# Output projection by seven products of half-size blocks in place of eight

## The chip, the cores and the metric

The kernel runs on one core of a Trainium2 chip. The metric is the device time of one execution in microseconds. The engines of the core are called here as in the profile: PE (TensorE, with PEld for its weight loads), DVE (VectorE), ACT (ScalarE), POOL (GpSimd) and SP (SyncE, which issues all DMAs of this kernel).

## The reference, cut to what matters

The kernel computes one decoder layer on a sequence of 4096 rows of 1024 float32 values. Two branches, a sliding-window attention and a gated linear attention (GLA), each give 512 columns; their concatenation goes through one output projection with a 1024x1024 matrix and a residual with layer norm.

```python
mix = jnp.einsum('bse,ed->bsd', jnp.concatenate([out_a, out_b], axis=-1), w_out[layer])
x = layer_norm(ALPHA * x + mix, ln_g[layer], ln_b[layer])
```

## The kernel before

The 4096 rows are 32 tiles of 128 (`NB` is 32). Three stages run one after the other, each a loop over the tiles: attention, GLA, output. Every float32 operand of a projection is split into two parts in the format fp32r, a rounded high part (a cast, mostly on ACT) and the rest (a subtraction, mostly on DVE), and `project` makes three matmuls for each of its eight slices of 128 input columns: high by high, high by low and low by high.

The attention stage stores its transposed result per tile in DRAM as `mixd[n][0]` (L432), the GLA stage as `mixd[n][1]` (`b_store`, L714). The weights of a stage are loaded near the end of the stage before by `load_group`, split, and kept in places of SBUF by slot and slice: slot 0 holds the attention's `wq`, then the GLA's `v`; slot 1 `wkv`, then the GLA's `q`; slot 2 the two gates in turn; slot 3 the GLA's `k`, loaded at tile 2 of the attention stage. The two column halves of the output matrix are loaded in the last GLA tile into slots 0 and 2 (L751, L765).

In the output stage a tile is loaded from `mixd` with its residual rows `xr` and split (`mh` on ACT, `ml` on DVE). For each column half PE makes 24 matmuls of 128x512 into one PSUM bank `py`, DVE adds the residual and takes the statistics. Then DVE and ACT make the factor of the norm, ACT normalises, POOL multiplies by `lg`, DVE adds `lb`, and SP stores:

```python
act.activation(y, y, AF.Identity, bias=nb_, scale=rs)
pool.tensor_tensor(y, y, lg, ALU.mult)
dve.tensor_tensor(y, y, lb, ALU.add)
sp.dma_start(out[rows, :], y)
```

PE's order of matmuls within a GLA tile is written out by hand: the steps of other tiles (`b_attn`, `b_state`, `b_update`, `b_out`, `b_store`) stand between pieces of `project`. The order in each engine's queue is fixed when the kernel is built, by a planner that takes from the instructions that are ready by its own estimate the one with the highest priority, in general the one written first. Each queue is then worked off in that order, SP's as well. Tiles of a pool share its buffers, and a pool that is opened later may use the memory of one that was closed; an instruction that writes into such a place waits until the last use of what was there.

## Time and profile before

| | us |
|---|---|
| runs, median of 3 | 1720.0 (1718.03 to 1721.3) |
| the profiled execution | 1719.78 |
| its span, first to last instruction | 1718.1 |
| mean granted clock of PE | 0.997 |

The profile shows one execution. Times in its rows are counted from the start of the span. A group of instructions has its count, its busy time and the mean length of one; for matmuls the length is from issue to the end of the pipeline, and consecutive ones overlap. The attention stage takes about the first 655 us, the GLA stage runs to about 1353 us, and the output stage to the end.

### The profile page before, as it was taken

Reading aid. Unit: us, or ns where it says so; the run is one execution under the profiler, and the core shown is the slowest. Engines: PE = TensorE matmul, PEld = TensorE weight load, DVE = VectorE, ACT = ScalarE, POOL = GpSimd, SP = SyncE. Lnnn points to the kernel's source line nnn. Section 1 sums busy time; section 2 is a strip of 40 time slices with the busy share of each in tenths; the row PEclk is TensorE's granted clock in tenths of the full one; section 3 lists DMA queues with packets and bytes.
Section 4 is the critical chain, followed back from the end, with each engine's and each line's share of the span. In section 5 each row is a group of like instructions: output and inputs, shape, how many; then the busy total and the mean of one; then the engine's idle time right before and its main releaser. Section 6 shows DMA issues by size and latency. Waiting matters only on the chain.

```text
span 1718.1 us, 26157 instructions
## 1 busy us (share of the span) xinstructions
PE 1689.6 (98%) x9477; PEld 1445.5 (84%) x9477; DVE 1123.9 (65%) x2562; ACT 774.8 (45%) x2070; POOL 486.6 (28%) x623
## 2 busy tenths in 40 slices
PE   8999999999999998999999999999999899999998
PEld 7788888888888886888888888888888788888886
DVE  7777777777777786666666666666665755555555
ACT  6444344444344455555555555555555522222221
POOL 1333223333223355222222222222222422222221
PEclk9999999999999999999999999999999999999999
DMA  6211111111111131111111111111111444444442
GB/s 221 70 38 38 48 46 38 38 37 38 49 45 38 38 110 63 45 38 38 38 38 38 38 38 38 38 38 38 38 38 38 154 147 147 145 142 142 148 147 86
DMA packets 66389, 119.68 MB, mean 70 GB/s; under 512 B 22738, under 2 KB 27220, under 8 KB 66260
## 3 DMA queue, kind: packets, MB, share of 16 engines
q1 hardware_dynamic: 66260, 118.01, 21.6%
q8 instruction: 74, 1.21, 0.3%
q14 instruction: 55, 0.45, 0.1%
HBM read 84.37 MB, written 33.62 MB: 69 GB/s over the span
## 4 chain that ended last, share of the span: by engine, by line
PE 58%; DVE 1%; ACT 0%; issue 0%; POOL 0%; DVEq 0%
PE py L142 7%; PE py L144 7%; PE py L143 7%; PE bg L142 3%; PE bg L144 3%; PE bv L142 3%; PE bv L143 3%; PE bg L143 3%; PE bv L144 3%; PE bq L142 2%; PE bq L143 2%; PE bq L144 2%; PE bk L144 2%; PE bk L143 2%; PE bk L142 2%; PE to L719 1%
## 5 line engine op out<-in xcount | busy, mean ns | idle before, releaser
L394 POOL TENSOR_SCALAR_AFFINE_SELECT p<-hl 128x512 fp32r<-128x512 f32 x256 | 165.2, 681 | 385.9 <-ACT hl L388 351.7
L142 PE MATMUL py<-wh,mh 128*128 128x512 f32 x512 | 199.8, 390 | 0.0
L143 PE MATMUL py<-wl,mh 128*128 128x512 f32 x512 | 199.7, 390 | 0.0
L144 PE MATMUL py<-wh,ml 128*128 128x512 f32 x512 | 199.4, 390 | 0.0
L363 ACT ACTIVATE pr<-psc,ngm 128x128 f32<-128x128 f32 x256 | 90.5, 366 | 196.0 <-PE psc L344 138.1
L813 POOL TENSOR_TENSOR y<-y,lg 128x1024 f32<-128x1024 f32 x31 | 74.2, 2392 | 267.9 <-ACT y L812 267.9
L567 POOL TENSOR_TENSOR qp<-bqs,ee 128x256 f32<-128x256 f32 x32 | 23.7, 740 | 337.4 <-ACT ee L564 323.4
L144 PEld LDWEIGHTS py<-wh,ml 128*128 128x128 f32 x512 | 96.4, 188 | 20.1
L143 PEld LDWEIGHTS py<-wl,mh 128*128 128x128 f32 x512 | 96.4, 188 | 19.8
L142 PEld LDWEIGHTS py<-wh,mh 128*128 128x128 f32 x512 | 96.4, 188 | 19.7
L142 PE MATMUL pg<-wh,xh 128*128 128x512 f32 x256 | 110.8, 433 | 1.5 <-ACT wh L100 1.5
L142 PE MATMUL bg<-wh,xh 128*128 128x512 f32 x256 | 107.3, 419 | 0.0
L142 PE MATMUL bv<-wh,xh 128*128 128x512 f32 x256 | 103.8, 405 | 0.0
L100 ACT CAST mh<-mr 128x1024 fp32r<-128x1024 f32 x32 | 33.7, 1053 | 154.2 <-PE py L143 154.2
L142 PE MATMUL pq<-wh,xh 128*128 128x512 f32 x256 | 103.2, 404 | 0.0
L144 PE MATMUL bg<-wh,xl 128*128 128x512 f32 x256 | 101.2, 395 | 0.0
L144 PE MATMUL pg<-wh,xl 128*128 128x512 f32 x256 | 101.0, 395 | 0.0
L144 PE MATMUL pq<-wh,xl 128*128 128x512 f32 x256 | 101.0, 395 | 0.0
L143 PE MATMUL bv<-wl,xh 128*128 128x512 f32 x256 | 101.0, 395 | 0.0
L143 PE MATMUL bg<-wl,xh 128*128 128x512 f32 x256 | 100.8, 394 | 0.0
L143 PE MATMUL pq<-wl,xh 128*128 128x512 f32 x256 | 100.7, 393 | 0.0
L143 PE MATMUL pg<-wl,xh 128*128 128x512 f32 x256 | 100.3, 392 | 0.2 <-DVE wl L105 0.2
(225 smaller groups left out, 4897.1 us busy)
## 6 DMA issues: line engine op xcount, KB each, us to landing
xraw<-in_xt_dram SPq DMA_DIRECT2D x62, 512.0 KB
mr<-mx SPq DMA_DIRECT2D x64, 256.0 KB
xr<-in_xn_dram SPq DMA_DIRECT2D x32, 512.0 KB
out_dram<-y SPq DMA_DIRECT2D x31, 512.0 KB
mx<-att SPq DMA_DIRECT2D x32, 256.0 KB
mx<-mb SPq DMA_DIRECT2D x32, 256.0 KB
wraw<-in_w_a_dram SPq DMA_DIRECT2D x16, 256.0 KB
wraw<-in_w_b_dram SPq DMA_DIRECT2D x16, 256.0 KB
```

The lines of the kernel that those rows point to most:

```text
L100: act.copy(hdst, src)
L142: pe.matmul(dst[:, :n], a, hs[k][:, :n], start=(k == 0), stop=False)
L143: pe.matmul(dst[:, :n], a, ls[k][:, :n], start=False, stop=False)
L144: pe.matmul(dst[:, :n], b, hs[k][:, :n], start=False, stop=(k == NK - 1))
L363: act.activation(pr[:, i], sc[i], AF.Exp, bias=ngm[:, h : h + 1], scale=0.125, accum_out=den[:, h : h + 1])
L394: pool.affine_select(o, hl[:, i], [[0, 4], [sg_, P]], ALU.is_gt if b else ALU.is_ge, 0.0, base=0, channel_multiplier=-sg_,)
L567: pool.tensor_tensor(qp, B[n]["q"], ee, ALU.mult)
L719: pe.transpose(to[:, hs], og[:, hs], ident)
L813: pool.tensor_tensor(y, y, lg, ALU.mult)
```

## The change

The output projection is done for pairs of row tiles. Its left operand is cut into two row tiles by two halves of 512 input columns (a11 and a12 for the even tile, a21 and a22 for the odd one), the matrix into two by two blocks of 512x512, and the four result blocks come from seven block products (Strassen's scheme in Winograd's form) instead of eight. A product has 4 slices by 3 matmuls.

The sums of left blocks are made in the GLA stage: the attention stage stores a11 and a21 per pair, `b_rows` loads them back, `b_store` forms four combinations on DVE, and each of the seven operands of a pair goes to DRAM (`opd`). The seven combinations of the matrix blocks are made, split and stored to DRAM (`wod`) during the GLA stage in small steps of `w_prepare`, two steps per tile at a lower priority (the offset of -300), the rest at tile `NB - 3`. `w_fetch` loads them at the end into the places of the GLA's weights, and the seventh into a new pool.

In the output stage `step(p, t)` makes product t of pair p, and DVE adds the bank into the residual rows `y`. Products 0, 1, 2 and 5 accumulate one after another in bank `a`, which is read in between; 3 and 6 in `b`; 4 in `c`. Pairs 0 and 1 run interleaved product by product, the others one at a time. The norm of a tile is cut into pieces that run in the following steps; both the factor `lg` and the addition of `lb` are now on POOL, each in two halves. Stores are collected by `put` and issued by `flush` at the end of a GLA tile, or after the seventh step of a pair. The GLA's `q` and `k` weights are one load of 528 columns in slot 1, and some GLA buffers are shared or no longer doubled.

```diff
-                wb["q"] = load_group(wr, w_b, 0, 272, 1, 272)
-            if n == 2:
-                wb["k"] = load_group(wr, w_b, 272, 256, 3, 256)
+                wb["qk"] = load_group(wr, w_b, 0, 528, 1, 528)
...
-            qp = f1.tile([P, 256], F32, tag="qp", name=f"qp{n}")
-            pool.tensor_tensor(qp, B[n]["q"], ee, ALU.mult)
-            B[n]["qp"] = qp
+            pool.tensor_tensor(ee, B[n]["q"], ee, ALU.mult)
+            B[n]["qp"] = ee
...
-            kp = f1.tile([P, 256], F32, tag="kp", name=f"kp{n}")
-            dve.tensor_tensor(kp, pk[:, :256], B[n]["ff"], ALU.mult)
-            B[n]["kp"] = kp
+            ff = B[n]["ff"]
+            dve.tensor_tensor(ff, pk[:, :256], ff, ALU.mult)
+            B[n]["kp"] = ff
...
-            gw = b2.tile([P, 4, P], F32, tag="gw", name=f"gw{n}")
+            gw = b1.tile([P, 4, P], F32, tag="gw", name=f"gw{n}")
...
-            og = b1.tile([P, 512], F32, tag="og", name=f"og{n}")
+            og = om.rearrange("p h v -> p (h v)")
...
-            act.copy(mb, to)
-            sp.dma_start(mixd[n][1].rearrange("p a s -> p (a s)"), mb)
...
+            act.copy(mb, tof)
+            put(opd[p][4 + odd], mb)
+            a11, a21 = B[n - odd]["at"]
+            if not odd:
+
+                dve.tensor_tensor(a11, a11, a21, ALU.subtract)
+                put(opd[p][2], a11)
+                ax = b1.tile([P, 512], F32, tag="ax", name=f"ax{p}")
+                dve.tensor_tensor(ax, tof, a11, ALU.add)
+                B[n]["ax"] = ax
+                return
+            ax = B[n - 1]["ax"]
+            dve.tensor_tensor(a21, tof, a21, ALU.add)
+            put(opd[p][3], a21)
+            dve.tensor_tensor(a11, tof, a11, ALU.subtract)
+            put(opd[p][1], a11)
+            dve.tensor_tensor(ax, ax, tof, ALU.subtract)
+            put(opd[p][6], ax)
+
+        def b_rows(n):
+
+            if n % 2 == 0:
+                B[n]["at"] = []
+                for t, src in (("a11", opd[n // 2][0]), ("a21", a21d[n // 2])):
+                    a = b1.tile([P, 512], F32, tag=t, name=f"{t}_{n}")
+                    sp.dma_start(a, src)
+                    B[n]["at"].append(a)
...
+        def w_prepare(k, c):
...
+            def part(i, src):
+                w = b2.tile([P, 2, 256], F32R, tag="wo", name=f"wop{i}_{k}{c}")
+                split(w[:, 0], w[:, 1], src, act, dve)
+                puts_w.append((wod[i][k][:, :, 256 * c : 256 * c + 256], w.bitcast(F32)))
+
+            yield
+            part(0, r11)
+            dve.tensor_tensor(r11, r12, r11, ALU.subtract)
+            yield
...
+        def op_places(p):
+
+            a = xp.tile([P, NK, P], F32, tag="xraw", name=f"oa{p}").rearrange("p a s -> p (a s)").bitcast(F32R)
+            b = xp.tile([P, NK, P], F32R, tag="xh", name=f"ob{p}").rearrange("p a s -> p (a s)")
+            c = xp.tile([P, NK, P], F32R, tag="xl", name=f"oc{p}").rearrange("p a s -> p (a s)")
+            w = {0: (b[:, LO], a[:, LO]), 3: (b[:, HI], a[:, HI]), 1: (c[:, LO], c[:, HI])}
+            for i in w:
+                op_load(p, w, i)
+            return w
+
+        PLACE = {0: (0, 0), 3: (0, 4), 1: (1, 0), 4: (1, 4), 2: (2, 0), 6: (2, 4)}
+
+        def w_fetch(i, pool_=None):
+            for k in range(4):
...
+                sp.dma_start(w[:, :, :512].bitcast(F32), wod[i][k])
+                wo[i][k] = w
...
+            with tc.high_priority(offset=-300):
+                next(prep, None)
...
+            if last:
+                w_fetch(0)
+            if n == NB - 3:
+                for _ in prep:
+                    pass
...
-                wo[1] = load_group(wr, w_o, 512, 512, 2, 512)
+                ops = [op_places(p) for p in range(2)]
+                w_fetch(3)
+            flush(puts)
+            b_rows(n)
...
+        def split_op(w, i):
+            h, l = w[i]
+            act.copy(h, l.bitcast(F32))
+            dve.tensor_tensor(l, l.bitcast(F32), h, ALU.subtract)
+
+        def product(dst, w, i, more=False):
+
+            h_, l_ = w[i]
+            for k in range(4):
+                h, l = wo[i][k][:, 0, :512], wo[i][k][:, 1, :512]
+                a, b = h_[:, k * P : (k + 1) * P], l_[:, k * P : (k + 1) * P]
+                pe.matmul(dst, a, h, start=(not more and k == 0), stop=False, skip_group_check=more)
+                pe.matmul(dst, a, l, start=False, stop=False, skip_group_check=more)
+                pe.matmul(dst, b, h, start=False, stop=(k == 3), skip_group_check=more)
...
+            dve.bn_aggr(mv, st.rearrange("p a b -> p (a b)"))
+            dve.tensor_scalar(ms, ms, 1.0, EPS, ALU.mult, ALU.add)
+            log_(rs, ms)
+            act.activation(rs, rs, AF.Exp, scale=-0.5)
+            yield
+
+            dve.tensor_scalar(nt, rs, rs, -0.5, ALU.mult, ALU.mult)
+            dve.tensor_scalar(nt, nt, ms, 1.5, ALU.mult, ALU.add)
+            dve.tensor_scalar(r2, nt, rs, None, ALU.mult)
...
+            dve.tensor_scalar(nb_, mv[:, 0:1], r2, -1.0, ALU.mult, ALU.mult)
+            act.activation(y, y, AF.Identity, bias=nb_, scale=r2)
+            yield
+            for s in (LO, HI):
+                pool.tensor_tensor(y[:, s], y[:, s], lg[:, s], ALU.mult)
+            for s in (LO, HI):
+                pool.tensor_tensor(y[:, s], y[:, s], lb[:, s], ALU.add)
+            put(out[rows, :], y)
+
+        ORDER = (0, 3, 1, 4, 2, 6, 5)
+        ys = []
+        for i in (4, 2, 6, 5):
+            if i in (4, 2):
+                ys.append(load_rows(len(ys)))
+            if i == 4:
+                w_fetch(1)
+            for p in range(2):
+                op_more(p, ops[p], (i,))
+            w_fetch(i, c1 if i == 5 else None)
...
+        STEPS = (("a", 0, False), ("b", 3, False), ("a", 1, True), ("c", 4, False), ("a", 2, True), ("b", 6, True), ("a", 5, True))
...
+            x, op, more = STEPS[t]
+            product(b[x], ops[p], op, more)
+            i, half, first = READS[t]
+            y, s = ys[p][i], (LO, HI)[half]
+            if first:
+                dve.scalar_tensor_tensor(y[:, s], y[:, s], ALPHA, b[x], ALU.mult, ALU.add)
+            else:
+                dve.tensor_tensor(y[:, s], y[:, s], b[x], ALU.add)
+            if t in (3, 4, 5, 6):
+                dve.bn_stats(st[i][:, half, :], y[:, s])
+            run_later()
+            if t in (5, 6):
+                g = normed(2 * p + i, y, st[i], p == pairs - 1 and i == 1)
+                next(g)
+                later.append(g)
...
+        for group in [(0, 1)] + [(p,) for p in range(2, pairs)]:
+            for t in range(7):
+                for p in group:
+                    step(p, t)
+
+                    if p + 2 < pairs and t == 2:
+                        ops[p + 2] = op_places(p + 2)
+                    elif p + 2 < pairs and t > 2:
+                        op_more(p + 2, ops[p + 2], ORDER[t : t + 1])
+                nxt = group[-1] + 1
+                if t == 6:
+                    flush(puts)
...
+                ready = range(7)[t : t + 1] if nxt > 2 else ((), (), (), (), (0, 1, 2), (3,), (4, 5, 6))[t]
+                for i in ready:
+                    split_op(ops[nxt], ORDER[i])
```

## Rows read from the trace of the kernel before

**Rows 1.** The page, part 1: busy us, share of the span, instructions

```profile
PE 1689.6 (98%) x9477; PEld 1445.5 (84%) x9477; DVE 1123.9 (65%) x2562; ACT 774.8 (45%) x2070; POOL 486.6 (28%) x623
```

**Rows 2.** Windows of one GLA tile and one output tile: busy time by engine

```profile
core 0: us, PE busy (x) PEld busy (x) DVE busy (x) ACT busy (x) POOL busy (x), PEclk, DMA share, GB/s
999.47:1021.03 21.56, 21.56 (x136) 19.02 (x135) 13.02 (x32) 11.83 (x29) 5.48 (x7) 1.00 0.11 37
...
1503.16:1514.04 10.88, 10.88 (x49) 9.01 (x48) 5.93 (x13) 2.70 (x5) 2.39 (x1) 1.00 0.43 146
```

**Rows 3.** Groups of instructions by shape, window 1345 to 1718, the output stage

```profile
L142 PE MATMUL py<-wh,mh 128*128 128x512 f32 x512 | 199.8, 390 | 0.0
...
L797 DVE BATCH_NORM_STATS2 cst<-y 128x6 f32<-128x512 f32 x64 | 44.2, 690 | 1.2
L796 DVE SCALAR_TENSOR_TENSOR y<-xr,py 128x512 f32<-128x512 f32 x64 | 44.0, 687 | 78.5 <-PE py L144 78.4
...
L798 DVE BATCH_NORM_AGGREGATE mv<-cst 128x2 f32<-128x12 f32 x32 | 6.4, 201 | 0.1
...
L825 DVE SCALAR_TENSOR_TENSOR crs<-cnt,crs 128x1 f32<-128x1 f32 x32 | 5.1, 160 | 1.1
```

**Rows 4.** Timeline of PE: start us, length us, then what; last `bv`, `bg`, `py`

```profile
1338.41 0.39 PE L144 MATMUL bv<-wh,xl 128*128 128x512 f32 x1
...
1344.91 1.11 PE L719 MATMUL to<-cs,og 128*128 128x128 f32 x4 [1.62 <-DVE og L709]
...
1351.79 0.39 PE L144 MATMUL bg<-wh,xl 128*128 128x512 f32 x1
...
1353.74 0.40 PE L142 MATMUL py<-wh,mh 128*128 128x512 f32 x1
...
1709.45 0.39 PE L144 MATMUL py<-wh,ml 128*128 128x512 f32 x1
```

**Rows 5.** Windows with DMA share and GB/s; the page's 40 slices in GB/s

```profile
5.00:10.00 5.00, 5.00 (x17) 3.92 (x16) 3.77 (x8) 3.34 (x8) 0.00 (x0) 1.00 0.98 342
...
1345.00:1350.00 5.00, 5.00 (x16) 3.72 (x17) 2.93 (x7) 4.10 (x9) 2.20 (x3) 0.66 0.57 194
...
GB/s 221 70 38 38 48 46 38 38 37 38 49 45 38 38 110 63 45 38 38 38 38 38 38 38 38 38 38 38 38 38 38 154 147 147 145 142 142 148 147 86
```

**Rows 6.** Instructions of single lines: duration ns min/median/max, first and last start

```profile
L105 DVE TENSOR_TENSOR al<-am,ah x32: 674/674/1775, 688.2 to 1358.5; 128x512 fp32r<-128x512 f32 x32
...
L576 DVE TENSOR_TENSOR dd<-sm,sm x31: 151/153/1033, 702.9 to 1355.8; 128x2 f32<-128x2 f32 x31
...
L671 POOL TENSOR_TENSOR gw<-gw,gs x32: 1290/1296/1599, 681.1 to 1358.1; 128x512 f32<-128x512 f32 x32
```

**Rows 7.** Timelines of DVE and POOL at two places: start us, length us

```profile
1358.51 1.77 DVE L105 TENSOR_TENSOR al<-am,ah 128x512 fp32r<-128x512 f32 x1
...
1358.14 1.60 POOL L671 TENSOR_TENSOR gw<-gw,gs 128x512 f32<-128x512 f32 x1 [1.36 <-ACT gs L664]
...
1508.60 0.69 DVE L796 SCALAR_TENSOR_TENSOR y<-xr,py 128x512 f32<-128x512 f32 x1 [1.35 <-PE py L144]
...
1508.60 2.39 POOL L813 TENSOR_TENSOR y<-y,lg 128x1024 f32<-128x1024 f32 x1 [8.48 <-ACT y L812]
```

**Rows 8.** Groups and waits of 28 GLA tiles, window 700 to 1300

```profile
L105 DVE TENSOR_TENSOR lal<-la,lah 128x256 fp32r<-128x256 f32 x28 | 11.7, 416 | 0.0
...
PEld tr L524 <- DVE r L517: 9.7, 28, 0.4
```

**Rows 9.** Timelines of DVE and SP at the end of the span

```profile
1713.41 1.42 DVE L807 SCALAR_TENSOR_TENSOR y<-y,crs,lb 128x512 f32<-128x512 f32 x2
...
1714.19 1.00 SPq L808 DMA_DIRECT2D out_dram<-y  x2
```

**Rows 10.** Timelines of DVE and PE at the turn into the GLA stage

```profile
648.90 1.74 DVE L369 TENSOR_TENSOR pr<-pr,rec 128x512 f32<-128x512 f32 x1
...
650.79 0.63 PE L384 MATMUL pt<-cs,pr 128*128 128x128 f32 x4 [2.30 <-DVE pr L369]
```

More of the change, by code (lines that the diff above doesn't have):

```diff
@@ L88, in bank @@
         return ps.tile([P, 512], F32, tag=tag, name=name)
-    mixd = [
-        [dr.tile([P, 4, P], F32, tag=f"mx{n}_{h}", name=f"mx{n}_{h}") for h in range(2)]
-        for n in range(NB)
+    opd = [
+        [dr.tile([P, 512], F32, tag=f"op{p}_{i}", name=f"op{p}_{i}") for i in range(7)]
+        for p in range(NB // 2)
+    ]
+    a21d = [dr.tile([P, 512], F32, tag=f"a21_{p}", name=f"a21_{p}") for p in range(NB // 2)]
+    wod = [
+        [dr.tile([P, 2, 512], F32, tag=f"wo{i}_{k}", name=f"wod{i}_{k}") for k in range(4)]
+        for i in range(7)
     ]
@@ new lines, in layer_kernel, with put, flush @@
+        puts, puts_w = [], []
+        def put(dst, src):
+            puts.append((dst, src))
+        def flush(which):
+            for dst, src in which:
+                sp.dma_start(dst, src)
+            which.clear()
+        def w_prepare(k, c):
+            q = []
+            for i in range(2):
+                for j in range(2):
+                    r = wr.tile([P, 256], F32, tag="wraw", name=f"wo{k}_{c}{i}{j}")
+                    sp.dma_start(r, w_o[k + 4 * i, :, 512 * j + 256 * c : 512 * j + 256 * c + 256])
+                    q.append(r)
+            r11, r12, r21, r22 = q
+            def part(i, src):
[6 more added lines that the diff above has]
+            yield
+            dve.tensor_tensor(r12, r22, r12, ALU.subtract)
+            part(6, r22)
+            yield
+            dve.tensor_tensor(r22, r22, r11, ALU.subtract)
+            part(3, r11)
+            yield
+            part(4, r21)
+            dve.tensor_tensor(r21, r21, r22, ALU.subtract)
+            yield
+            part(2, r12)
+            yield
+            part(1, r22)
+            yield
+            part(5, r21)
+            yield
@@ new lines, in w_all, with op_load @@
+        def w_all():
+            for k in range(4):
+                for c in range(2):
+                    for _ in w_prepare(k, c):
+                        yield
+                        flush(puts_w)
+            yield
+        prep = w_all()
+        wo = [[None] * 4 for _ in range(7)]
+        LO, HI = slice(0, 512), slice(512, 1024)
+        latest = [None]
+        def op_load(p, w, i):
+            latest[0] = sp.dma_start(w[i][1].bitcast(F32), opd[p][i]).ins
+        def op_places(p):
[6 more added lines that the diff above has]
+            return w
@@ L763, in layer_kernel @@
             b_gate(n, pg)
+            with tc.high_priority(offset=-300):
+                next(prep, None)
             if last:
-                wo[1] = load_group(wr, w_o, 512, 512, 2, 512)
+                ops = [op_places(p) for p in range(2)]
+                w_fetch(3)
+            flush(puts)
+            b_rows(n)
         b_attn(NB - 1)
@@ L775, in layer_kernel, with op_more @@
         c2 = pcx.enter_context(tc.tile_pool(name="c2", bufs=2))
+        c4 = pcx.enter_context(tc.tile_pool(name="c4", bufs=6))
+        def op_more(p, w, which=(4, 2, 6, 5)):
+            for i in which:
+                h = c2.tile([P, 512], F32R, tag=f"oh{i}", name=f"oh{i}_{p}")
+                l = c2.tile([P, 512], F32R, tag=f"ol{i}", name=f"ol{i}_{p}")
+                w[i] = h, l
+                op_load(p, w, i)
+        def split_op(w, i):
+            h, l = w[i]
+            act.copy(h, l.bitcast(F32))
+            dve.tensor_tensor(l, l.bitcast(F32), h, ALU.subtract)
@@ new lines, in layer_kernel, with run_later @@
+        for i in ORDER:
+            for p in range(2):
+                split_op(ops[p], i)
+        pairs, later = NB // 2, []
+        def run_later():
+            for g in list(later):
+                if next(g, 0) == 0:
+                    later.remove(g)
+        STEPS = (("a", 0, False), ("b", 3, False), ("a", 1, True), ("c", 4, False), ("a", 2, True), ("b", 6, True), ("a", 5, True))
+        READS = ((0, 0, True), (1, 1, True), (0, 1, True), (0, 0, False), (1, 1, False), (0, 1, False), (1, 0, True))
@@ new lines, in layer_kernel, with step @@
+        state = {}
+        def step(p, t):
+            if t == 0:
+                b = {x: bank(g, f"p{x}{p}") for x, g in (("a", "pj"), ("b", "c"), ("c", "d"))}
+                st = [c2.tile([P, 2, 6], F32, tag=f"st{i}", name=f"cst{2 * p + i}") for i in range(2)]
+                state[p] = b, st
+            b, st = state[p]
+            x, op, more = STEPS[t]
[4 more added lines that the diff above has]
+                dve.scalar_tensor_tensor(y[:, s], y[:, s], ALPHA, b[x], ALU.mult, ALU.add)
+            else:
+                dve.tensor_tensor(y[:, s], y[:, s], b[x], ALU.add)
[6 more added lines that the diff above has]
+                later.append(g)
@@ L818, in rsqrt_eps @@
+        while later:
+            run_later()
+        flush(puts)
 def rsqrt_eps(act, dve, log_, ms, rs, nt, scale):
```

110 lines of the change are left out of this document (53 added, 57 removed).

## Prediction, on record before the changed kernel was run

> **What bounds the kernel now.** I read the totals first. TensorE (PE) is busy in 98% of the span, VectorE (DVE) in 65%, the others in less [rows 1]. A mean hides the stages, so next come the windows of one tile in each stage. One tile of the GLA stage takes 21.56 us, one of the output stage 10.88 us; PE fills both without a gap, while DVE works 13.02 us of the first and 5.93 us of the second [rows 2]. So in both stages the time is the number of matmuls times their distance. In the output stage that is 10.88 / 48 = 0.2267 us for a 128x512 matmul; the 0.39 us in its group [rows 3] is latency, since matmuls overlap, and must not be used for sums. From the first `py` matmul at 1353.74 to the last at 1709.45 are 355.9 us with that one's own 0.23, of which 1536 x 0.2267 = 348.2 us are matmuls; 7.7 us are idle time, a slow clock and the last GLA tile's matmuls in between [rows 4].
>
> **Part 1, seven products for eight.** A pair of row tiles now costs 7 x 12 = 84 matmuls of the same shape for 96: 192 fewer in all, 192 x 0.2267 = **-43.5 us**. A pair is then 84 x 0.2267 = 19.04 us long. That is all of the gain that I can find; the rest of the change costs.
>
> **Part 2, DVE in the output stage.** Per pair: 7 splits of 128x512 (0.674 each, the usual `al` split [rows 6]), 7 reads of a bank (0.687), 4 statistics (0.690), and per tile one aggregate (0.201) and five scalars (about 0.160) [rows 3]: 4.7 + 4.8 + 2.8 + 2.0 = 14.3 us of 19.04, against 2 x 5.93 = 11.9 of 21.76 now. On throughput DVE stays under PE. ScalarE and POOL too: POOL gets 8 operations of 128x512 at 1.296 us [rows 6], 10.4 us per pair.
>
> But the trace shows that POOL and DVE hold each other up. A split with both inputs in SBUF began 0.37 us after a POOL operation and took 1.77 us instead of 0.674: it ended when POOL had ended and one short operation more. A 128x2 addition, normally 0.153 us, once took 1.033. The read of a PSUM bank beside a POOL operation kept its 0.69 us [rows 6, 7]. So of the work above only the 7 splits, and perhaps the scalars, can be held, each split by at most 1.775 - 0.674 = 1.1 us. POOL is busy 10.4 / 19.04 = 54% of the time, so I expect 7 x 0.54 x 0.55 = 2.1 us of holds: DVE 16.4 us of 19.04. The new POOL operations are halves, which keeps a hold short.
>
> [...]
>
> What a late DVE costs: bank `a` is read after products 0, 2 and 4 and written again by the next product but one, so a read has one product, 2.72 us, to finish. The heaviest step is the seventh: read, statistics, aggregate, nine scalars and a split with a hold, 0.69 + 0.69 + 0.20 + 1.44 + 0.67 + 1.1 = 4.8 us. It leaves 2.1 us of backlog, and the next pair's first read ends 2.1 + 0.69 = 2.8 us after its product: about nothing to spare. I take 0.4 us of PE idle per pair, 14 x 0.4 = **+5.6 us** for pairs 2 to 15. Bounds: 0, and, if DVE lost all of POOL's 10.4 us, 14 x (14.3 + 10.4 - 19.04) = +79.
>
> **Part 3, the turn into the output stage.** Before, 4 MB of weights were loaded and split there. Now seven prepared operands come from DRAM, 2.10 MB each, 14.7 MB, all into places that free up at the end: the first when the last `bv` matmul is through, 1338.6, the next after `bk`, the others after `bg` (1352.2) or later [rows 4]. Ahead of the last of them SP also asks for 14 row operands of two pairs (3.7 MB), two pairs of residual rows (2.1 MB) and the last six stores (1.6 MB): 22.0 MB. The DMA engines moved at most 342 GB/s, at a busy share of 0.98 [rows 5]. At that rate the last operand lands at 1338.6 + 64.4 = 1403.0; the last quarter product of pair 0 and the last product of pair 1 follow, 3.4 us: 1406.4. PE unhindered would end these 14 products at 1353.7 + 38.1 + 7.7 = 1399.5. So even a saturated queue costs 6.9 us. The queue will have gaps, since SP issues in order, waits for places, and spends about 0.5 us per issue [rows 9]. I take nine tenths, 308 GB/s: 71.5 us, end at 1413.5, **+14.0 us**. Bounds: 0, if I misjudge which places are free, and +42 at 221 GB/s, the busiest slice of the page [rows 5] (99.6 us, end at 1441.6). [...]
>
> **Part 4, the GLA stage.** It gets six DVE additions of 128x512 per pair in `b_store` (about 2.0 us per tile) and the preparation of the weights: 56 splits and 32 subtractions of 128x256, 88 x 0.416 = 36.6 us of DVE, 1.3 us per tile, and 56 casts on ACT [rows 8]. DVE goes from 13.0 to 16.3 us of 21.56. PE covers that, unless an added operation is in front of one that PE waits for. There is such a place: PE waits 9.7 us in 28 tiles for `r` already [rows 8]. SP gets some 180 issues more, none of which delays `sd`, as stores are asked for after their data are made. I take **+4 us** in all, bounds 0 and +18 (0.6 us, one added operation, in each of 30 tiles). The in-place `qp`, `kp`, `og` and the single `gw` free nothing and wait for nothing: each is read by TensorE before the next tile writes it.
>
> **Part 5, the turn into the GLA stage.** `qk` is now one load of 528 columns near the end of the attention stage; the `k` half was loaded early before. Four DVE and four POOL splits of 256 columns more come where DVE is already late: the weight splits on POOL hold DVE there, `pr` took 1.74 us and PE stood 2.30 us for it [rows 10]. **+2 us**, between 0 (the early load is saved) and +4.
>
> **Part 6, the end.** The last tile but one takes four POOL operations, 5.2 us, that end about 7.1 us after PE; its 512 KB store then lands some 3 us later. Now the last DVE operations begin at 1713.41 and the last stores are issued from 1714.19, 4.5 us after PE's end, and the span ends at 1718.1 [rows 9]. **+2 us**, 0 to +4.
>
> **The sum.** -43.5 + 5.6 + 14.0 + 4 + 2 + 2 = -15.9 us. The profiled execution took 1719.8 us (span 1718.1), 0.2 below the median of the runs, so **1704 us**, 0.9% faster. What is removed besides the matmuls (the casts of `mh`, the `lb` addition on DVE, DVE's 3.8 us waits for POOL at the end) lay beside PE and is worth nothing.
>
> **Rivals.** *The loads hide* (chance 0.13): places free earlier than I read, or PE is later than I think; part 3 is then 0 and the time 1690. For it: the DMA engines were idle most of the GLA stage. Against it: the 22 MB have a start that no order can pull ahead of 1338.6. *The loads are slower* (0.09): +42 for +14, 1732. For it: the first slice of the page, also many loads of weights, managed 221 GB/s. Against it: that slice waited for raw places, and its full windows ran at 342. *DVE is held by POOL* (0.12): if all seven splits and one scalar (0.88 more) are held to the full, DVE takes 14.3 + 7.7 + 0.9 = 22.9 us per pair; PE waits 3.9 us in each of 14 pairs, +54 for +5.6: 1752. That is slower than before, and it decides from 6.5 us of holds per pair on: 4.7 us of slack, and 14 x 1.8 = 25 us that bring 1698.4 (the sum without part 2) to 1723.4. For it: the order in each queue is fixed at build time, and a hold it didn't plan for pushes everything behind it. Against it: POOL is idle 46% of the time, and a split that finds it idle isn't held. *DVE crowds the GLA stage* (0.10): +18 for +4, 1718. *The forecast* (0.56): 1704, itself within 1692 to 1715.
>
> **Range and chances.** I give 1684 to 1722: the forecast, the hidden loads and the crowded GLA stage, without the two slow rivals (0.21). A change of 0.2%, 3.4 us, is about what a measurement of this kernel tells from none. Faster by more: the forecast, the hidden loads and part of the crowded stage, 0.73. Within it: the rest of that, 0.06. Slower: the two slow rivals, 0.21.
>
> **What would show it.** In the profile after: 1344 product matmuls 0.2267 us apart; a pair at 19.0 to 19.8 us; DMA at 300 GB/s or more and PE idle between products from about 1360 to 1415, then no more; splits in the output stage between 0.67 and 1.8 us long; a GLA tile within 21.6 to 22.0 us. I am wrong if a pair takes over 20.5 us (then DVE is the bound), if PE is idle less than 5 or more than 30 us in the first two pairs, or if a GLA tile has grown by 0.5 us.

## The result and the profile after

The changed kernel takes 1798.7 us (median of 4 runs, 1796.3 to 1800.7) and the kernel before 1720.5 (4 runs, 1718.0 to 1721.3): a ratio of 1.0456, interval 1.0438 to 1.0475, so 78 us slower where 1704 us was forecast. The profiled execution has a span of 1799.0 us, against 1718.1 before [rows 1].

The page of the changed kernel, its part 1 and the row of PE in part 2 (one figure for each fortieth of the span, in tenths):

```profile
PE 1679.3 (93%) x9285; PEld 1422.6 (79%) x9285; DVE 1251.6 (70%) x2815; ACT 813.1 (45%) x2182; POOL 576.0 (32%) x704
...
PE   8999999999999989999999999999999688888876
```

PE has 192 matmuls less, as the change promises, but it now stands still: 93% busy for 98%, and the run of digits below 9 lies at the end. No other engine is near 100%, neither on this page nor in the last 14 pairs below. So no engine became the bound; something makes PE wait.

Windows of the changed kernel, in order: the first eight GLA tiles, one odd and one even later tile, the first two pairs of the output stage (14 products), the other 14 pairs (98 products), and three short windows behind a gap (columns as in [rows 2]):

```profile
646.97:849.82 202.85, 186.79 (x1100) 157.69 (x1098) 161.17 (x374) 118.59 (x315) 59.76 (x79) 0.99 0.50 158
1048.73:1071.54 22.81, 21.88 (x135) 19.06 (x134) 14.46 (x34) 11.98 (x30) 5.42 (x7) 1.00 0.25 75
1071.54:1093.08 21.54, 21.54 (x135) 19.01 (x134) 14.91 (x35) 11.84 (x30) 5.50 (x7) 1.00 0.21 69
1383.43:1446.18 62.75, 43.76 (x188) 34.46 (x187) 36.11 (x75) 19.64 (x40) 3.53 (x4) 0.86 0.90 334
1446.18:1785.00 338.82, 289.53 (x1177) 231.45 (x1175) 203.91 (x414) 95.02 (x175) 167.37 (x120) 0.93 0.45 153
1549.61:1551.70 2.09, 2.09 (x5) 1.70 (x6) 1.59 (x3) 0.54 (x2) 2.09 (x2) 0.50 0.00 0
1551.70:1554.40 2.70, 2.70 (x9) 2.08 (x9) 1.05 (x4) 1.24 (x1) 2.70 (x3) 0.62 0.00 0
1554.40:1557.20 2.80, 2.80 (x14) 2.28 (x13) 0.69 (x1) 0.00 (x0) 2.80 (x3) 1.00 0.51 174
```

Split at the starts of the `bq` products and of the output products, the two spans differ so:

| piece, us | before | after | difference | forecast |
|---|---|---|---|---|
| to the first `bq` | 642.9 | 647.0 | +4.1 | +2 |
| first to last `bq` (31 GLA tiles) | 682.8 | 712.1 | +29.4 | +4 |
| last `bq` to the first output product | 28.1 | 24.3 | -3.8 | 0 |
| output products, first to last | 355.9 | 401.6 | +45.7 | -23.9 |
| behind the last product | 8.4 | 14.0 | +5.6 | +2 |

Four stretches carry it. The first eight GLA tiles take 202.9 us (186.7 before). From the tenth on, the tiles take 21.5 and 22.8 us in turn (21.57 each before). The first two pairs take 62.8 us, with one gap of 17.1 us. The other 98 products take 338.8 us for the 98 x 2.72 = 266.6 of the forecast, although DVE is busy in only 203.9 of them.

In these last pairs the pattern repeats every two pairs: 4.1 to 5.6 us of idle PE before the third product (1.5 in the first pair of the 14), then half the clock for a while (the granted clock is 0.50 in the window behind the gap, 1.00 five microseconds later), and 0.6 to 4.9 us before seven of the 14 seventh products. So the mean of 24.2 us per pair hides two kinds: the pairs 2, 4, 6 and so on take 26 to 33 us, those between them 19.2 to 19.9, close to the 19.0 to 19.8 forecast for all. One such stretch, in timelines of POOL, SP, ACT, DVE and PE of the changed kernel (start us, length us, engine, line, operation; in brackets the idle time before it and who ended it):

```profile
1529.94 3.45 POOL L962 TENSOR_TENSOR y<-y,lg 128x512 f32<-128x512 f32 x2
1533.34 3.00 POOL L964 TENSOR_TENSOR y<-y,lb 128x512 f32<-128x512 f32 x2
...
1536.36 0.34 SPq L763 DMA_DIRECT2D out_dram<-y  x1
1536.81 0.37 SPq L819 DMA_DIRECT2D ol<-op  x1
1537.27 2.44 SPq L930 DMA_DIRECT2D y<-in_xn_dram  x2
1539.81 1.32 SPq L819 DMA_DIRECT2D ol<-op  x3
...
1540.50 0.62 ACT L913 CAST oh<-ol 128x512 fp32r<-128x512 f32 x1 [6.08 <-DMA ol<-op]
...
1541.15 0.69 DVE L914 TENSOR_TENSOR ol<-ol,oh 128x512 fp32r<-128x512 f32 x1 [5.36 <-ACT oh L913]
...
1548.78 0.68 DVE L1009 SCALAR_TENSOR_TENSOR y<-y,pa 128x512 f32<-128x512 f32 x1
...
1549.61 0.77 PE L922 MATMUL pa<-wo,oc 128*128 128x512 f32 x1 [5.22 <-ACT crs L497]
```

Read it from the top. POOL ends `lb` for a row tile of pair 4 at 1536.34. SP's next transfer, the store of that tile, has stood in its queue waiting for it; behind it stand the operand loads of pair 7 and two loads of residual rows, which in turn wait for such a store to land. Over the whole run SP stands 128.8 us in 30 such waits for POOL. ACT has waited 6.1 us for an operand, DVE 5.4 us for ACT, for a split that PE needs only some 12 products later; and behind that split in DVE's queue stands the read of bank `a` (L1009) that PE waits for. The releaser in PE's bracket, `crs` on ACT, had long been done; the late one is the bank read. This is theory A: **SP's in-order queue**. Rival B: DVE is late because **POOL holds it**. Rival C: the planner simply put the splits too far ahead.

### The profile page after: what moved, and what is told of

Same layout as the page of the kernel before. It is cut to its first block, busy times and chain, and to the rows that moved or that the text cites. A ratio compares the mean times of both kernels' runs of the same rounds, so it can differ in the third digit from the quotient of the medians.

```text
span 1799.0 us, 26851 instructions
## 1 busy us (share of the span) xinstructions
PE 1679.3 (93%) x9285; PEld 1422.6 (79%) x9285; DVE 1251.6 (70%) x2815; ACT 813.1 (45%) x2182; POOL 576.0 (32%) x704
## 4 chain that ended last, share of the span: by engine, by line
PE 28%; DVE 10%; DMA 9%; POOL 6%; ACT 3%; issue 3%; SPq 1%; POOLq 0%; ACTq 0%; DVEq 0%
POOL y L962 3%; DMA ol<-op 2%; PE bg L149 2%; PE bg L150 2%; PE bg L151 2%; PE bv L149 2%; PE bv L150 2%; PE bv L151 2%; DMA wod<-wop 2%; DMA out_dram<-y 2%; POOL y L964 2%; PE bk L150 1%; PE bk L151 1%; PE bk L149 1%; PE pa L922 1%
## 5 line engine op out<-in xcount | busy, mean ns | idle before, releaser
L962 POOL TENSOR_TENSOR y<-y,lg 128x512 f32<-128x512 f32 x62 | 92.4, 1511 | 229.8 <-ACT y L959 216.4
L149 PE MATMUL pg<-w,xh 128*128 128x512 f32 x256 | 111.0, 434 | 1.6 <-ACT w L107 1.5
L149 PE MATMUL bg<-w,xh 128*128 128x512 f32 x256 | 105.8, 413 | 0.0
L149 PE MATMUL bv<-w,xh 128*128 128x512 f32 x256 | 103.8, 406 | 0.0
L149 PE MATMUL pq<-w,xh 128*128 128x512 f32 x256 | 102.5, 401 | 0.0
L112 DVE TENSOR_TENSOR xl<-xraw,xh 128x512 fp32r<-128x512 f32 (+1 forms) x132 | 96.4, 749 | 7.9 <-POOL xh L109 3.8
L151 PE MATMUL pg<-w,xl 128*128 128x512 f32 x256 | 101.4, 396 | 0.0
L151 PE MATMUL pq<-w,xl 128*128 128x512 f32 x256 | 101.2, 395 | 0.0
L150 PE MATMUL pg<-w,xh 128*128 128x512 f32 x256 | 100.6, 394 | 0.2 <-DVE w L112 0.2
L150 PE MATMUL bv<-w,xh 128*128 128x512 f32 x256 | 100.7, 394 | 0.0
L151 PE MATMUL bv<-w,xl 128*128 128x512 f32 x256 | 100.7, 393 | 0.0
L150 PE MATMUL pq<-w,xh 128*128 128x512 f32 x256 | 100.5, 393 | 0.0
L151 PE MATMUL bg<-w,xl 128*128 128x512 f32 x256 | 100.4, 392 | 0.0
L150 PE MATMUL bg<-w,xh 128*128 128x512 f32 x256 | 100.3, 392 | 0.0
```

The source lines that it names most:

```text
L112: leng.tensor_tensor(ldst, src, hdst, ALU.subtract)
L149: pe.matmul(dst[:, :n], a, hs[k][:, c], start=(k == 0), stop=False)
L150: pe.matmul(dst[:, :n], a, ls[k][:, c], start=False, stop=False)
L151: pe.matmul(dst[:, :n], b, hs[k][:, c], start=False, stop=(k == NK - 1))
L962: pool.tensor_tensor(y[:, s], y[:, s], lg[:, s], ALU.mult)
```

## Experiments in the output stage

**Transfers that wait, moved to POOL's queue (e1), and the stores alone (e2).**

```diff
-                    flush(puts)
+                    flush(puts, pool)       # e1, e2: finished rows are stored from POOL's queue
...
-                sp.dma_start(y, xn[n * P : (n + 1) * P, :])
+                (sp if n < 4 else pool).dma_start(y, xn[n * P : (n + 1) * P, :])    # e1 alone
```

> The changed kernel, but in the output stage the stores of finished rows, and the loads of the residual rows from tile 4 on, are asked for from POOL's queue; SP's queue holds only the loads of operands. The order of the operations on PE, DVE and ACT stays, and POOL does the same passes by `lg` and `lb`. Theory A (operand loads stand in SP's in-order queue behind stores that wait for POOL, and behind residual rows that wait for such a store to land; ACT's casts and DVE's splits wait for the late loads, and DVE's bank reads, which PE waits for, stand behind the splits): the two gaps of some 5.6 and 2 to 5 us in every two pairs go, the last 98 products take 270 to 290 us in place of 338.8, and the whole takes 1730 to 1750 us. Rival B (DVE is held beside POOL's passes, so the splits and bank reads are late by themselves): the same passes run beside the same DVE operations, so the gaps stay and the time is within 10 us of 1799. Rival C (the planner put the splits of the pair after next too far ahead on DVE): the order on DVE is unchanged, so no gain either.

> The changed kernel, but only the stores of finished rows are asked for from POOL's queue; the loads of residual rows stay on SP, each of them still in wait for the store of the row that had its buffer to land. Theory A with the stores as the part that matters: as the run that moves both, 1730 to 1750 us. Theory A with the residual rows as the part that matters: they now wait on SP in the store's place, and the time stays at 1785 to 1800 us. Rival B and rival C: within 10 us of 1799.

Measured: e1 1779.8 us (ratio to before 1.0348, 1.0330 to 1.0365), e2 1806.8 (1.0499, 1.0484 to 1.0515). Both miss theory A's numbers; e2 lies within those of B and C, e1 within nobody's. In e1 the gap before the third product is gone from the fourth pair on, as A wants, but one of 1.6 to 2.9 us before the seventh now stands in nearly every pair, as B wants. Why, two views of e1 show: the DVE splits of one kind (min, median and max in ns), and timelines of POOL, DVE and PE:

```profile
L914 DVE TENSOR_TENSOR oa<-oa,ob x32: 668/960/6058, 1358.9 to 1714.4; 128x512 fp32r<-128x512 f32 x32
```

```profile
1685.42 0.60 POOL L763 DMA_DIRECT2D out_dram<-y  x1 [0.30 <-POOL y L964]
1686.05 2.55 POOL L962 TENSOR_TENSOR y<-y,lg 128x512 f32<-128x512 f32 x2
1688.54 2.54 POOL L964 TENSOR_TENSOR y<-y,lb 128x512 f32<-128x512 f32 x2
...
1684.71 6.93 DVE L914 TENSOR_TENSOR oa<-oa,ob 128x512 fp32r<-128x512 f32 x2 [0.84 <-ACT ob L913]
1691.56 0.68 DVE L1011 TENSOR_TENSOR y<-y,pc 128x512 f32<-128x512 f32 x1
...
1694.17 0.47 PE L922 MATMUL pa<-wo,oh 128*128 128x512 f32 x1 [2.77 <-DVE y L1011]
```

One split of 0.68 us lasted 6.0 us, until POOL had ended four passes; 13 splits of e1 and 12 of e2 lasted over 4 us, while none in the changed kernel lasted over 1.8. The edit brought a cost of its own, so these two runs don't decide between A and B. It also did two things that weren't meant: the planner set DVE's splits of the first pairs later, and the last four operand stores of the GLA stage went to POOL's queue as well (more on this at e7). In e2 the residual rows took the stores' place on SP (the load of a row waits there for a store that POOL asks for), which fits A's second half. SP's waits over the whole run, the first two of the changed kernel, then one of e2 and one of e5, the next experiment (us in total, times, longest):

```profile
SPq L763 <- POOL y L964: 128.8, 30, 6.5
SPq L930 <- DMA out_dram<-y: 35.5, 19, 3.5
...
SPq L930 <- DMA out_dram<-y: 121.5, 24, 9.9
...
SPq L763 <- POOL y L966: 40.8, 9, 6.5
```

**The same order on SP without POOL (e5).** The stores of finished rows stay on SP, behind the last operand load that was asked for before them:

```diff
-                    flush(puts)
+                    flush(puts, latest[0] if nxt > 3 else None)   # the store's place on SP: behind that load
```

> The changed kernel, but from the third group of the output stage on the stores of finished rows stand on SP behind the last operand load that was asked for before them, and the residual rows that wait for such a store stand behind it; POOL issues no transfer. The two runs that put these transfers on POOL's queue brought a cost of their own: a DVE split that begins beside POOL's issue was held for 6.0 us, through four passes of POOL. Here that cause is away. Theory A (SP's order alone made the operand loads, the splits and the bank reads late): the gaps before the products t = 2 and t = 6 both go, the last 98 products take 272 to 295 us in place of 338.8, and the whole takes 1738 to 1760 us. Rival B (DVE is held beside POOL whatever SP does): gaps of 2 to 4 us before t = 6 stay in every pair and the whole takes 1770 to 1790 us.

Measured: 1744.4 us (1.0147, 1.0130 to 1.0163), 54 us less. The window of the last 98 products of e5, and its splits of the same kind:

```profile
1449.46:1733.10 283.64, 272.80 (x1177) 221.03 (x1175) 218.07 (x414) 96.14 (x175) 172.37 (x120) 0.99 0.54 183
```

```profile
L916 DVE TENSOR_TENSOR oa<-oa,ob x32: 684/1013/1842, 1362.8 to 1687.2; 128x512 fp32r<-128x512 f32 x32
```

283.6 us in place of 338.8: the gaps before the third product are gone, seven of 1.1 to 3.5 us remain (one of 1.6 before a third product, the others before a seventh). POOL's passes and DVE's operations are those of the changed kernel, and the splits were even held longer beside POOL: 42 us in all over 0.675 us each, for 26 in the changed kernel. So theory A is shown for 55 us of the stage, and B is left with the rest. Which part of A counts, the stores or the residual rows behind them, isn't told apart: e5 moved both. Rival C falls as the whole cause: the order on DVE hardly changed, and the splits stand 11 or 12 bank reads ahead, as they did. Whether a shorter lead would have removed the gaps as well was not tried.

**The first two pairs (e7).** There PE stood 17.1 us before the fifth product. SP and DVE of the changed kernel:

```profile
1398.01 4.13 SPq L819 DMA_DIRECT2D oa<-op  x4
1403.13 0.32 SPq L763 DMA_DIRECT2D op<-mb  x1
1404.43 1.60 SPq L763 DMA_DIRECT2D op<-a  x2
1406.99 0.32 SPq L763 DMA_DIRECT2D op<-ax  x1
1412.16 0.81 SPq L930 DMA_DIRECT2D y<-in_xn_dram  x2
...
1398.15 0.68 DVE L743 TENSOR_TENSOR ax<-ax,to 128x512 f32<-128x512 f32 x1
...
1416.14 0.69 DVE L1009 SCALAR_TENSOR_TENSOR y<-y,pa 128x512 f32<-128x512 f32 x1 [5.24 <-DMA y<-in_xn_dram]
```

The last operand store's data is made at 1398.8, but it is asked for at 1407.0, behind weights; the residual rows, which take over the memory of the GLA stage, can only be asked for when it has landed. The edit puts the fetches of two of the seven weights behind the rows:

```diff
+                if i in (2, 6):
+                    after(f.ins, rows_in[0])        # f: the fetch of weight i; rows_in: the last load of rows
```

> The changed kernel, but on SP the fetches of the weights of products 2 and 6 (4 MB) stand behind the loads of the residual rows of the first two pairs and so behind the last operand stores of the GLA stage. Theory H (the wait of 17.3 us before the fifth product is for the rows, which were asked for only at 1412.2, behind 4 MB of weights and five stores; the transfers run at their full rate meanwhile): the rows come some 10 us sooner, the wait falls to 5 to 9 us, and the whole takes 1788 to 1792 us. Rival I (the weights that now come later are the next to be waited for): the gap moves to the products that read them (the ninth to twelfth) and the whole stays at 1796 to 1800 us.

Measured: 1786.3 us (1.0385, 1.0368 to 1.0403), 12 us less and more than expected as a whole, but the wait itself fell less than H forecast: the gap before the fifth product went from 17.1 to 11.0 us, not to 5 to 9, and the first 14 products from 62.8 to 57.2. The other 8.8 us came off the later pairs, where the planner also changed PE's order of products; that part was not followed up. In e1 and e2 the last four operand stores had left SP's queue (in e1 POOL asked for them at 1396.1 to 1398.5 us, where SP did at 1403.1 to 1407.3), 20 weight fetches stood before the rows in place of 24, and the same gap was 9.2 and 9.1 us. That fits H: what stands before the rows on SP delays them. Rival I falls: no other gap appeared among the 14.

## Experiments in the GLA stage

Every other tile is 1.27 us longer. Timelines of SP and DVE of the changed kernel in such a tile, and one of PE's waits from 900 to 1300 us (us in total, times, longest):

```profile
1221.62 0.24 SPq L560 DMA_DIRECT2D sd<-r  x1
...
1222.96 1.45 SPq L763 DMA_DIRECT2D op<-a  x2
1224.68 0.32 SPq L763 DMA_DIRECT2D op<-ax  x1
1225.10 0.40 SPq L564 DMA_DIRECT2D sm<-sd  x1
...
1230.56 0.92 DVE L580 TENSOR_TENSOR dd<-sm,sm 128x2 f32<-128x2 f32 x1
1231.40 0.68 DVE L732 TENSOR_TENSOR a<-a,a 128x512 f32<-128x512 f32 x1
```

```profile
PEld bo L698 <- POOL sbl L590: 8.5, 9, 1.0
```

Two suspects stand in the chain that leads over `dd` and `st` to `sbl` and PE's `bo`: four operand stores ahead of the load of `sm` (one of `mb` before the three shown), and the subtraction L732 right behind `dd`. One edit for each:

```diff
-                dve.tensor_tensor(a11, a11, a21, ALU.subtract)                     # e3: behind om's additions
+                after(dve.tensor_tensor(a11, a11, a21, ALU.subtract).ins, B[n]["add"])
-            flush(puts)                                                            # e4: behind the load of sm
+            flush(puts, B[n]["smd"])
```

> The changed kernel, but in the GLA stage the subtraction a11 - a21 of every other tile is held on DVE until the two additions of `om` of that tile are done; nothing else changes. Theory D (this subtraction, planned between `dd` and the two products that make `st`, is what makes every other tile 1.27 us longer, 15 to 16 us over the stage): the tiles from the tenth on are all 21.5 us long and the whole takes 1782 to 1786 us. Rival E (the operand stores on SP in front of the load of `sm` make it): tiles stay at 21.5 and 22.8 us in turn, and the time is within 3 us of 1799.

> The changed kernel, but in the GLA stage the stores of operands stand on SP behind the load of `sm` of their tile; DVE's order of operations is left to the planner. Theory E (the stores that stand before the load of `sm` make `dd`, and with it `st`, `sbh`, `sbl` and PE's `bo`, late in every other tile): the tiles from the tenth on are all 21.5 us long and the whole takes 1782 to 1786 us. Rival D (the subtraction between `dd` and `st` makes it): tiles stay at 21.5 and 22.8 us in turn, and the time is within 3 us of 1799.

Measured: e3 1788.4 us (1.0393, 1.0377 to 1.0408), e4 1779.8 (1.0346, 1.0330 to 1.0361). e3 lies between its two forecasts: the long tiles shrink by half, to 22.2 us. With e4 they are gone, and the subtraction stands behind the product with `tot`, where DVE was idle until its rows came; two tiles of e4, of the kinds that were long and short:

```profile
1041.56:1063.09 21.53, 21.53 (x135) 19.00 (x134) 14.40 (x34) 11.84 (x30) 5.49 (x7) 1.00 0.28 98
1063.09:1084.62 21.53, 21.53 (x135) 19.00 (x134) 14.90 (x35) 11.84 (x30) 5.49 (x7) 1.00 0.15 50
```

So the four stores ahead of `sm` are the cause (E), and the subtraction adds to it only then. But `dd` did not wait for the load while the kernel ran: in none of these tiles was DVE idle before it. What changed is the plan. With the load later in SP's queue the planner puts `dd` behind the gate's operations on DVE, beside POOL's `gw`, where it took 0.92 us in place of 0.15; with e4 it stands ahead of them, as in the short tiles. The whole gained 19 us, a little more than expected, because the first tiles gained too (202.9 to 200.3 us).

**The three orders together (e8),** the edits of e4, e5 and e7:

> The changed kernel with three edits in the order on SP: operand stores behind the load of `sm`, stores of finished rows behind the operand loads, weights of products 2 and 6 behind the residual rows. If the three causes are apart (A, E and H): 1798.7 less 19 less 40 to 58 less 7 to 10 is 1712 to 1733 us. If DVE's holds beside POOL take over once SP's order is mended (B): 1750 to 1765 us.

Measured: 1719.0 us (0.9996, 0.9986 to 1.0005): the kernel before, within what can be told, and the forecast for three causes apart. Alone the three were worth 19, 54 and 12 us, 86 in all; together 80. What is left over the prediction's 1704 us lies in the first eight GLA tiles (200.2 us, 186.7 before), in the last 98 products (279.9 us, 7.7 more than the forecast's 266.6 + 5.6) and at the end (5.6 us for 2). The gap of 9.9 us in the first group lies within the 14 that were forecast there. One of the gaps that stay, in timelines of DVE and PE of e8: the split before the read was held beside POOL.

```profile
1521.77 1.72 DVE L918 TENSOR_TENSOR oc<-oc 128x512 fp32r<-128x512 f32 x1
1523.41 0.68 DVE L1015 TENSOR_TENSOR y<-y,pa 128x512 f32<-128x512 f32 x1
...
1524.23 0.47 PE L926 MATMUL pa<-wo,oh 128*128 128x512 f32 x1 [1.42 <-DVE y L1015]
```

**The weight preparation (e6, e9, e10, e12).** The planner packs it into the first eight tiles. e6 spreads it, each DVE operation behind the product by `nrm` of its tile; e9 leaves out its DVE work, e12 all its arithmetic; e10 puts it behind `lal`, where DVE is idle, asks for two steps at one place in a tile, and moves its stores behind the load of `sm`:

```diff
+            hold = lambda o: after(o.ins, gate[0])
...
-                split(w[:, 0], w[:, 1], src, act, dve)
+                act.copy(w[:, 0], src)
+                hold(dve.tensor_tensor(w[:, 1], src, w[:, 0], ALU.subtract))   # e6: gate = the product by nrm
+            gate[0] = dve.tensor_tensor(lal, la, lah, ALU.subtract).ins        # e10: gate = lal
+            flush(puts_w, B[n]["smd"])                                         # e10: its stores behind sm
```

> The kernel with the operand stores behind the load of `sm` (1779.8 us), and besides that the preparation of the weights is spread: each of its subtractions and splits on DVE is held behind the product by `nrm` of the tile in which the program asks for it, so that they lie in tiles 1 to 28 in place of 0 to 7. Theory F (the first eight tiles are 13.5 us longer than those of before because some eleven DVE operations and seven stores of the preparation fall into each; two or three in a tile find room): all tiles from the third on take 21.5 to 21.7 us and the whole takes 1764 to 1770 us. Rival G (each piece costs its time wherever it lies): the first eight tiles get shorter by what the later ones get longer, and the whole stays at 1776 to 1784 us.

> The kernel with the three edits together (1719.0 us), and DVE's part of the weight preparation left out: the 32 subtractions of weights and the 56 subtractions that make their low halves are gone (ACT copies both halves, so the products are taken with other weights); every load and store of the preparation stays. Theory K (the 88 DVE operations that fall into tiles 1 to 7 delay what PE waits for there; their transfers do not): tiles 3 to 8 take 21.5 to 21.9 us in place of 24.5 to 22.2, and the whole takes 1706 to 1710 us. Rival L (the preparation's 32 loads and 56 stores on SP, or ACT's casts, are the delay): those tiles keep at least half of their excess and the whole takes 1713 to 1720 us.

> The kernel with the three edits together (1719.0 us; its first eight tiles take 200.2 us, those of before 186.7), with all arithmetic of the weight preparation left out, on ACT as on DVE: the 56 stores take the loaded weights themselves, twice, so the products are taken with other weights; loads and stores keep their number and bytes. Without DVE's part alone the first eight tiles still took 197.0 us, but there ACT copied both halves. Rival L1 (the transfers, and their places before the load of `sm` on SP, are the rest): the eight tiles take 194 to 199 us and the whole 1712 to 1718 us. Theory L2 (ACT's casts, which stand in its queue before the copy for `r` and the exponentials, are the rest): the eight tiles take 187 to 189 us and the whole 1705 to 1708 us.

> The kernel with the three edits together (1719.0 us), and the weight preparation placed: on DVE each of its operations stands behind the making of `lal` of its tile, where DVE is idle for some 1.5 us until PE's sums come (1184.1 to 1185.6 and 1205.6 to 1207.1 us in the run with the three edits), two steps (at most four operations of 0.42 us) a tile; its stores stand on SP behind the load of `sm`. Theory K' (what counts is where in a tile DVE's extra operations fall): all tiles from the third on take 21.5 to 21.7 us and the whole takes 1706 to 1711 us. Rival G (each piece costs its time wherever it lies, as when they were spread behind the product by `nrm`): 1716 to 1725 us.

Measured: e6 1792.5 us (1.0425, 1.0410 to 1.0441), 13 us worse than e4; e9 1716.9 (0.9977, 0.9965 to 0.9989); e12 1710.0 (0.9942, 0.9925 to 0.9959); e10 1710.9 (0.9942, 0.9927 to 0.9957). The first eight tiles of e8, e9, e12 and e10, in that order:

```profile
645.82:846.07 200.25, 185.24 (x1100) 157.67 (x1098) 160.18 (x374) 118.14 (x315) 60.05 (x79) 0.99 0.50 159
```

```profile
647.98:844.97 196.99, 183.32 (x1099) 157.14 (x1098) 130.44 (x286) 131.94 (x371) 59.57 (x79) 0.99 0.50 161
```

```profile
647.13:837.26 190.13, 181.77 (x1099) 157.39 (x1098) 128.63 (x286) 101.53 (x259) 58.62 (x79) 0.99 0.51 167
```

```profile
647.16:834.56 187.40, 181.49 (x1100) 156.82 (x1099) 135.74 (x308) 105.85 (x273) 58.62 (x79) 0.99 0.28 94
```

Theory K, that DVE's operations are the delay, falls as put: without them 3.3 of the 13.5 us came back, though ACT's second copy may have taken part of it. (The changed kernel, e1, e2, e5 and e7, which have the same order in these tiles, took 201.6 to 204.9 us for them, so 3.3 is not far above the scatter.) With ACT's work gone too, 10.1 came back; the transfers, packed still tighter, kept 3.4. e12 ended between its two forecasts, nearer to L2: the arithmetic on ACT and DVE is the larger part, the transfers the smaller, and how the first divides between the two engines isn't shown. What settles the price is e10, as its theory K' forecast: all 31 tiles take 684.5 us there, 1.7 more than before, with the whole preparation in them; in e8 they took 695.4. The places on DVE, the pace and the places of the stores changed together there, so their shares aren't told apart. e6 missed both its forecasts: spread as well, but over the start of the tile, the preparation delayed the chain to `lal`; PE's weight loads waited for `lal` 15.2 us in 20 tiles (700 to 1300 us), and the 31 tiles took 706.7 us. Theory F, that a few operations in a tile find room anywhere, falls with it; Rival G, that they cost the same everywhere, falls with e10.

**The last rows (e11),** e10 with both last row tiles normed on DVE:

```diff
-                g = normed(2 * p + i, y, st[i], p == pairs - 1 and i == 1)
+                g = normed(2 * p + i, y, st[i], p == pairs - 1)
```

> As the run before, and besides the last pair's first 128 rows are scaled by `lg` and `lb` on DVE as its last 128 are, in place of ACT's norm and four passes of POOL (1705.2 to 1711.6 us in the run with the three edits, the store being asked for at 1711.7). Theory M (those passes are what ends last): 3 to 4 us less than the run before, 1702 to 1708 us in all. Rival N (DVE then does eight passes after the last product in place of four and ends no sooner): within 1 us of the run before.

Measured: 1705.1 us, ratio 0.9911 (0.9897 to 0.9926), 5.8 us less than e10, more than the 3 to 4 that theory M forecast. In the profiles the stretch behind the last product went from 14.3 to 10.2 us, so 4.2 us are the end and theory M holds; the rest lies in the output products, where the plan is the same but for the end, and was not followed up. The end of e8 on POOL and the end of e11 on DVE:

```profile
1705.21 3.09 POOL L966 TENSOR_TENSOR y<-y,lg 128x512 f32<-128x512 f32 x2 [9.14 <-ACT y L963]
1708.26 3.37 POOL L968 TENSOR_TENSOR y<-y,lb 128x512 f32<-128x512 f32 x2
```

```profile
1698.13 1.42 DVE L961 SCALAR_TENSOR_TENSOR y<-y,cr,lb 128x512 f32<-128x512 f32 x2
```

With PE's end at 1702.6 in e8, POOL's passes ended 9.0 us later, in e11 (PE's end 1692.6) DVE's last pass 7.0 us later, and DVE's passes no longer stand beside POOL's. So five edits, four to the order in the queues and one that moves work from ACT and POOL to DVE, take 93.6 us off the changed kernel and leave it 0.9% faster than the kernel before, with the same products. Its pieces against before: +4.9 to the first `bq`, +2.3 in the GLA tiles, -3.8, -20.6 in the output products, +1.8 at the end. That is the size that was forecast, 1704 us, but not for the kernel that was forecast.

## Why the prediction was wrong, by its own steps

**Part 1 held.** Matmuls of a running product lie 0.2267 us apart, and 43.5 us of PE work are gone: in e11 the whole output stage takes 335.3 us; the forecast of its parts 1 to 3 makes 355.9 - 23.9 = 332.0.

**Part 2 failed by what it left out.** It took a late DVE to be the only thing that can make PE wait, and reckoned DVE's load: 16.4 us per pair with holds. That was right in size (223.7 / 14 = 16.0 in a window of e8's last 98 products, 1422.61 to 1702.55). It never followed the stores. They were asked for "a step or a pair later", and the prediction took that to be late enough; but SP came to the stores before POOL's passes had ended, and behind the waiting store stood loads, casts, splits and at last a bank read. 55 us of the 78 are this. Without it the last 98 products cost 280 to 284 us, 13 to 17 over 266.6 for the +5.6 forecast: there the mechanism was right (reads behind held splits, as in the gap of e8 at 1524.23) and the size off: 0.96 us per pair in e8 for the 0.4 taken. Of e8's 13 us, 5 lie in the first two of these pairs, where PE waited for a cast and a split as well.

**Part 3 had nearly the right length for an incomplete reason.** It forecast 59.8 us for the first 14 products (38.1 + 7.7 + 14.0), from bandwidth; 62.8 were measured, at 334 GB/s and a DMA share of 0.90. But the gap came as one wait, for residual rows that stood behind weights needed later and behind the operand stores. The prediction counted their bytes and not their place: moving 4 MB behind them took 5.6 us off these products. That 62.8 came so near to 59.8 is partly luck.

**Part 4 failed in one sentence:** "SP gets some 180 issues more, none of which delays `sd`, as stores are asked for after their data are made." The stores came to stand ahead of the load of `sm`, which follows `sd`, and the planner then put `dd` late on DVE: 19 us. It also spread the preparation evenly, "1.3 us per tile", where the planner put it all into eight tiles, 16 us over before. In the order of e10 it could be had for almost nothing. Two counts were off, without much effect: `b_store` makes five additions per pair, not six, and SP got 236 issues more, not 180 (679 for 443). The stage grew by 29.4 us, past the +18 that the prediction gave as the bound and to its rival "DVE crowds the GLA stage".

**Parts 5 and 6** were small and too small: +4.1 for +2, and +5.6 for +2. At the end the last four POOL passes ran beside DVE's and took 6.4 us in place of the 5.2 reckoned; they ended 9.0 us after PE for 7.1, and the span ended 4.9 us behind them for some 3.

**The rivals.** The measured time lies above those of all of them. The prediction's signs of being wrong did show: a GLA tile grew by 0.95 us on the mean (limit 0.5), and a pair took 24.2 (338.8 / 14; limit 20.5). But the second sign was said to mean that DVE is the bound, and it was not: DVE was busy 14.6 us per pair (203.9 / 14), and e5 took 55 us off with longer holds. The sign would have confirmed the wrong cause. In the changed kernel no split took longer than 1.8 us, the longest that the prediction looked for; in e1 and e2, 25 splits were held for longer, over three or four POOL instructions.

What stays open: why moving the weights also took 8.8 us off the later pairs, whether the stores or the residual rows behind them count for more in e5, how the preparation's delay divides between ACT, DVE and the transfers, and the gap in the first group, 9.9 us in e8 and 9.7 in e11 (no form of it was tried in which the rows don't need the GLA stage's memory).

## What to carry to other kernels

Follow every transfer that waits down its issuing queue: list what stands behind it, and who waits for that, as far as PE; here stores that waited for POOL, and the loads that stood behind them, made 55 us (e5 against the changed kernel). Cost moved or added work by its place in each in-order queue, not by its mean per tile: with the same preparation in different orders the GLA stage grew by 2, 13 or 24 us in e10, e8 and e6 (31 tiles at 684.5, 695.4 and 706.7 us for 682.8). Where a planner fixes the order, look at what a moved transfer does to the plan, and not only at who waits for it. And before a bound is put down to an engine, compare its busy time per period with the period: here DVE was the last to release PE and was itself idle 40% of the time.

## What the runs showed of the hardware

In e1 and e2, in which POOL also issued transfers, splits on DVE, with both inputs in SBUF, were held for much longer than one POOL instruction: 25 of them took 4.3 to 6.1 us for the usual 0.68, through three or four passes of 1.29 us without a pause. With the same passes and no transfer from POOL, in the changed kernel and e5, the longest split was 1.8 us: DVE got in after the pass beside which the split had begun, and the pass behind took 1.75 us. Why DVE gets in between passes in the one case and not in the other, these runs don't show.

An idle PE paid twice here: after the 5.2 us without work before 1549.61 in the changed kernel, the granted clock was 0.50 in the next 2.1 us and 0.62 on the mean of the 2.7 after that, and the first product behind the gap took 4.8 us in place of 2.72.
